# Expert gate sums as one fp32 product per token and half, and the low parts of the down weights on VectorE

## The chip, the cores and the metric

The kernel runs on one core of a Trainium2 chip. The metric is the device time of one execution in microseconds; 2326.19 us is the median of three runs of the kernel before, from 2315.31 to 2331.83. The core has TensorE (matrix products into PSUM), VectorE, ScalarE and GpSimd (element-wise work on 128 partitions), SyncE (which here starts most transfers) and DMA engines.

## The reference, cut to what matters

The program computes two transformer blocks on 256 tokens of width 1024. The first block has an attention branch and a state-space branch, and then a layer of experts; the second block has neighbourhood attention, a gated recurrence and feed-forward layers. The change lies in the layer of experts and in nothing else:

```python
def peer_ffn(xn, w_q, keys1, keys2, u_tab, v_tab):
    q = (xt @ w_q).reshape(T, PEER_HEADS, PEER_QDIM)
    s1 = jnp.einsum('thd,hkd->thk', q[..., :half], keys1)
    s2 = jnp.einsum('thd,hkd->thk', q[..., half:], keys2)
    v1, i1 = lax.top_k(s1, PEER_TOPK)
    v2, i2 = lax.top_k(s2, PEER_TOPK)
    cand = v1[..., :, None] + v2[..., None, :]
    cidx = i1[..., :, None] * PEER_NKEYS + i2[..., None, :]
    sv, pos = lax.top_k(cand, PEER_TOPK)
    eidx = jnp.take_along_axis(cidx, pos, axis=-1)
    gw = jax.nn.softmax(sv, axis=-1)
    ...
    act = jnp.einsum('td,thkd->thk', xc, jnp.take(u_tab, ec, axis=0))
    hact = jax.nn.gelu(act, approximate=False) * gc
    return jnp.einsum('thk,thkd->td', hact, jnp.take(v_tab, ec, axis=0))
```

Each of 8 heads picks 16 of 128 x 128 = 16384 experts for each token, with weights gw. An expert is a row of u_tab and a row of v_tab.

## The kernel before, in words

The kernel does not gather experts. It computes the activations of all 16384 experts for all 256 tokens, multiplies each by the sum of the weights with which the token picked it (zero for most), and multiplies the result by all of v_tab. The experts are numbered (i1, i2); the tile A holds the activations as [i2, i1, token], in two halves of i1 with 64 values each.

The steps of the layer are these.

- The selection (`topk`) finds on VectorE the indices i1 and i2 and the weight of each of the 128 picks (8 heads x 16) of each token. At its end TensorE transposes them, so that the picks lie on partitions; `iT` holds i1, i2 and the weight, as three bf16 parts whose sum is the weight.
- The up part (`u_blocks`) takes one block of 128 experts after the other, 128 blocks. SyncE loads 512 KB of u_tab; ScalarE makes the high part of each weight (`whi`, line 1024), and VectorE or GpSimd the low part (`wlo`, line 1025); TensorE runs 24 products of 256 columns (high by high, high by low, low by high for eight chunks, lines 227 to 229); ScalarE applies the gelu (line 1037).
- The gate sums (`gates(half)`, lines 999 to 1015) run in 32 steps of 8 tokens for each half. For each token the sum over picks is a product of two matrices: one has a one where a pick's i2 equals the row (`oa`, line 1004), the other the weight where the pick's i1 equals the column (`ob`). VectorE compares a repeated index `iox` with i2 (128x1024, line 1004) and with i1 (128x512, line 1005, tile `eqw`), and multiplies the second by each of the three parts of the weight (line 1008, three times). TensorE then adds three bf16 products of 64 columns for each of 8 tokens (line 1012), and VectorE multiplies the sums into A (line 1014). `oa` has two buffers (one inside the tile C8, so that the trace calls it C), `ob` two, and the sums two banks of PSUM.
- The down part (`v_blocks`) goes over 128 blocks again. SyncE loads 512 KB of v_tab, ScalarE makes `whi` (line 1045), VectorE or GpSimd `wlo` (line 1046, by the set POOL_V), and the activations of the block are split in the same way: `wwh` on ScalarE (line 217) and `wwl` on VectorE (line 222), 256 columns each, with two buffers. TensorE runs 12 products of 512 columns for a block (lines 308, 309 and 312); those of line 312 read `wwl`. `wraw`, `whi` and `wlo` have three buffers each, and a block's weights are split two blocks ahead.
- Beside all this stand the modulation sums of the second block (`ada`, line 180): products of 128x1024 on VectorE with a sum along the row.

The order on each engine is not written by hand. The program is written step after step, with `even` dealing the steps of the selection, of the gate sums and of the modulation among the blocks; a scheduler of the build then puts the instructions of each engine into one queue by its own estimate of when each is ready. Each engine runs its queue in order. The gate sums of the first half (`gates(0)`) are dealt among up blocks 76 to 127, those of the second half (`gates(1)`) among the first 64 down blocks:

```python
    for i, _ in enumerate(u_blocks(76, 128)):
        even(g0, i, 32, 50)
...
    for i, _ in enumerate(v_blocks(0, 64)):
        even(g1, i, 32, 60)
        even(ada1, i, 40, 64)
```

In the queues the first gate step stands well ahead of up block 76, since the selection is expected to end earlier.

The names P, V, S, G and Q are TensorE, VectorE, ScalarE, GpSimd and SyncE.

Of the kernel before, what the change touches and what calls it, by code (L numbers as in the profile page):

```python
# [14 lines left out]
OP = mybir.AluOpType  # L15
# [9 lines left out]
def constants():  # L25
    """Arrays that depend on shapes alone."""
# [27 lines left out]
# Parameter vectors that are used as columns of 128: name, input, columns  # L54
# [6 lines left out]
def tiles(w, n=256):  # L61
    """w [R, C] in blocks of 512 rows and n columns, [C / n, R / 512, 128, 4 n]: rows of a block in four chunks of 128"""
    r, c = w.shape
    return w.reshape(r // 512, 4, 128, c // n, n).transpose(3, 0, 2, 1, 4).reshape(c // n, r // 512, 128, 4 * n)


def lay_out(inputs):
    """The inputs, in the order in which they are loaded"""
# [16 lines left out]
def program(tc, I, out, C, taps=None, upto=99):  # L85
# [44 lines left out]
    def col(name, i=0, n=1):  # L130
        """Column i.. of a parameter; a digit or two after the name picks the row of a stacked one."""
# [13 lines left out]
    def prepare_cols():  # L145
# [5 lines left out]
        # half the convolution: silu(y) = y / 2 (1 + tanh y / 2)  # L151
# [5 lines left out]
    msc = cst.tile([128, 5, 8], F32, name="msc")             # (1 + scale) * norm weight  # L157
    mods = cst.tile([128, 14, 8], F32, name="mods")      # layer 0: 0..5, layer 1: 6..11, context: 12, 13

    def ada(chunks, cs, raws, junk=None):  # L160
        """chunks of (layer, chunk, [(slot, which)]): mods[:, slot] = silu(c) @ ada_w chunk + ada_b chunk, as columns.
        cs(which): silu(c) as a row on all partitions"""
# [26 lines left out]
    def to_row(slot, src):  # L189
        """Columns src [128, 8] also as a row"""  # L190
# [7 lines left out]
    def row(dst, slot):  # L198
        """The row on all partitions"""
        Q.dma_start(dst, bass.AP(tensor=rowed[slot].tensor, offset=0, ap=[[0, 128], [1, D]]))  # L200
# [5 lines left out]
    pool_every = [0, 0]                                  # every n-th weight unit has its low part made by GpSimd  # L206

    after = []                                           # weights are split after these
# [22 lines left out]
    # Streamed weights: units of [128, 1024]; a phase may add buffers of its own to the rotation.  # L231
# [23 lines left out]
    def load_up(W, c0, u0=0):  # L255
        """Columns c0.. of W in tiles: two units of [128, 4, n]."""
# [10 lines left out]
    def load_dn(W, k0, gate=None, n=2, bufs=()):  # L267
        """Rows 128 k0 .. of W [K, 1024], with its columns times the gate: n units of [128, 1024]."""
# [11 lines left out]
    def up_T(units, cg, h, ps, k0=0, nk=8, start=True, stop=True):  # L280
        """ps[128 cols, 256 t] += W[:, cg].T @ h^T"""
# [6 lines left out]
    def up_N(units, tt, h, ps):  # L288
        """ps[128 t, 256 cols] = h @ W[:, 256 cols]"""
# [5 lines left out]
    def down(units, hk, acc, start, stop, free=False, tts=(0, 1), norm=None):  # L295
        """acc[tt][half][128 t, 512] += h^T[k].T @ W[k rows, 1024] for the units and their (hi, lo) [128, 256].
        At the stop the sums are finished one after the other, and the norm of them begins between.
        Free: the sums go on growing after they were read."""
# [40 lines left out]
    def start_acc(acc, x, ident):  # L339
        """Opens the sums with the residual x [128, 2, 1024]."""  # L340
# [7 lines left out]
    def rsqrt(v, mul, add):  # L348
        """v [128, n] -> 1 / sqrt(v * mul + add), in place"""
# [11 lines left out]
    def warm(src):  # L361
        """Has ScalarE's table for Sqrt loaded once src is there."""
# [4 lines left out]
    def keep_clock(ins=None, n=12):  # L367
        """Work without a result after ins: the tensor engine's clock falls when it waits."""
# [7 lines left out]
    class Norm:  # L376
        """src(tt, half) [128, 512] natural -> h = (hi, lo) [128, 8, 256] of (rms(x) * scale + shift)^T, in steps"""
# [6 lines left out]
        def stat(self, tt, hf):  # L384
            """Sums of squares"""
# [43 lines left out]
    class Output(Norm):  # L429
        """The final norm"""  # L430
# [14 lines left out]
    def nat_T(src, h, nchunk, scale=None):  # L445
        """src(tt, c) [128 t, 128] -> h = (hi, lo) [128, nchunk, 256]"""
# [13 lines left out]
    def mix(main, side, per=1):  # L460
        """Emit steps of side between the steps of main."""
# [1261 lines left out]
```

## Time and profile before

| what | value |
|---|---|
| median of three runs | 2326.19 us |
| lowest and highest run | 2315.31 and 2331.83 us |
| span of the profiled execution | 2330.2 us |
| TensorE busy (matmul) | 2223.8 us, 95% of the span |
| VectorE busy | 1678.7 us, 72% |
| ScalarE busy | 1013.8 us, 44% |
| GpSimd busy | 919.8 us, 39% |

The profile is of one execution; its span goes from the first to the last instruction. PE stands for TensorE's products, PEld for its weight loads, DVE for VectorE, ACT for ScalarE, POOL for GpSimd and SPq for SyncE's queue. L1012 is line 1012 of the kernel before. A product's duration in the profile holds the time it takes to pass through the array, so that the products of a run overlap; what one costs is read from the distance of two starts. An fp32 product stands in the trace as two records, each with a weight load of its own, where one in the reduced fp32 form (fp32r) or in bf16 has one. An instruction's time can include a wait for access that no semaphore shows.

### The profile page before, as it was taken

What the parts mean: (1) busy time and instruction counts of PE and PEld (TensorE: products, weight loads), DVE (VectorE), ACT (ScalarE), POOL (GpSimd) and SP (SyncE); (2) the same over time, 40 slices, a digit from 0 to 9 for tenths busy, and PEclk for the clock granted to TensorE, in tenths of its full rate; (3) what the DMA queues carried; (4) which work ended last, traced back from release to release, by engine and by line L of the source; (5) the groups of instructions that cost most, each with busy time, mean ns of one, the idle gap of its engine ahead of it and who ended that gap; (6) DMA issues with size and microseconds to landing.
All of it is one profiled execution on the core that took longest, in us unless ns stands there. A gap on an engine that the chain in (4) does not pass through costs nothing.

```text
span 2330.2 us, 39435 instructions
## 1 busy us (share of the span) xinstructions
PE 2223.8 (95%) x15750; PEld 2048.7 (88%) x15750; DVE 1678.7 (72%) x2726; ACT 1013.8 (44%) x1666; POOL 919.8 (39%) x439
## 2 busy tenths in 40 slices
PE   9999999998789999999999999999988899999999
PEld 8999998898789999997888877789977799888998
DVE  6677688699996553439887698643677687777876
ACT  5555664443234332223333345544542455444554
POOL 2222342205456533324434443442242355353654
PEclk9999999999899999999999999999999999999999
DMA  6544443566456543336555587775521555554552
GB/s 202 165 127 139 156 132 110 175 196 202 147 175 204 188 146 108 109 111 241 174 188 190 194 320 263 244 163 102 82 83 46 190 184 196 177 185 135 191 200 99
DMA packets 108218, 386.90 MB, mean 166 GB/s; under 512 B 13026, under 2 KB 14066, under 8 KB 108035
## 3 DMA queue, kind: packets, MB, share of 16 engines
q1 hardware_dynamic: 106080, 380.04, 48.8%
q0 software_dynamic: 1520, 3.75, 2.6%
q8 instruction: 123, 2.02, 0.3%
q10 hardware_dynamic: 434, 0.59, 0.1%
q14 instruction: 61, 0.49, 0.1%
HBM read 382.18 MB, written 2.16 MB: 165 GB/s over the span
## 4 chain that ended last, share of the span: by engine, by line
PE 73%; DVE 16%; DMA 4%; issue 3%; ACT 2%; POOL 1%; SPq 0%; ACTq 0%; DVEq 0%; POOLq 0%
PE mm L227 14%; PE mm L228 13%; PE mm L229 13%; PE tr L1012 7%; PE acc L312 6%; PE acc L309 5%; PE acc L308 5%; DVE A L180 2%; DMA wraw<-in_peer_v 2%; DVE wlox L222 1%; DVE xdt L180 1%; POOL wlo L1046 1%; DMA xdt<-in_ada_w 1%; DVE ob L1008 1%; PE acc L227 1%
## 5 line engine op out<-in xcount | busy, mean ns | idle before, releaser
L229 PE MATMUL mm<-xdt,wlo 128*128 128x256 f32 x1248 | 363.8, 292 | 29.6 <-DVE wlo L1025 29.2
L227 PE MATMUL mm<-xdt,whi 128*128 128x256 f32 x1248 | 370.6, 298 | 5.0 <-ACT A L1037 3.5
L1025 POOL TENSOR_TENSOR wlo<-wraw,whi 128x1024 fp32r<-128x1024 f32 x93 | 237.2, 2554 | 325.2 <-ACT whi L1024 323.2
L228 PE MATMUL mm<-xdt,whi 128*128 128x256 f32 x1152 | 336.8, 292 | 0.2 <-DVE xdt L418 0.2
L1046 POOL TENSOR_TENSOR wlo<-wraw,whi 128x1024 fp32r<-128x1024 f32 x80 | 208.6, 2609 | 288.2 <-ACT whi L1045 270.2
L1024 ACT ACTIVATE whi<-wraw 128x1024 fp32r<-128x1024 f32 x128 | 136.0, 1062 | 337.7 <-PE mm L228 156.3
L229 PEld LDWEIGHTS mm<-xdt,wlo 128*128 128x128 f32 x1248 | 249.9, 200 | 30.8 <-DVE wlo L1025 30.2
L227 PEld LDWEIGHTS mm<-xdt,whi 128*128 128x128 f32 x1248 | 250.6, 201 | 6.5 <-ACT A L1037 4.2
L228 PEld LDWEIGHTS mm<-xdt,whi 128*128 128x128 f32 x1152 | 231.2, 201 | 0.4 <-DVE xdt L418 0.4
L222 POOL TENSOR_TENSOR wlo<-wraw,whi 128x1024 fp32r<-128x1024 f32 x37 | 93.8, 2536 | 277.9 <-ACT whi L217 241.2
L309 PE MATMUL acc<-wlo,wwh 128*128 128x512 f32 x512 | 175.1, 409 | 3.2 <-DVE wlo L1046 2.5
L308 PE MATMUL acc<-whi,wwh 128*128 128x512 f32 x512 | 167.0, 410 | 1.1 <-ACT whi L1045 1.1
L312 PE MATMUL acc<-whi,wwl 128*128 128x512 f32 x512 | 158.1, 406 | 9.5 <-DVE wwl L222 9.4
L222 DVE TENSOR_TENSOR wlo<-wraw,whi 128x1024 fp32r<-128x1024 f32 x87 | 130.8, 1504 | 50.2 <-ACT whi L217 49.6
L1045 ACT ACTIVATE whi<-wraw 128x1024 fp32r<-128x1024 f32 x128 | 135.9, 1062 | 69.9 <-DMA wraw<-in_peer_v 40.4
L227 PE MATMUL mm<-F,whix 128*128 128x256 f32 x560 | 158.3, 283 | 8.0 <-ACT whix L217 5.7
L217 ACT ACTIVATE whi<-wraw 128x1024 fp32r<-128x1024 f32 x124 | 130.7, 1055 | 72.0 <-PE mm L228 35.4
L228 PE MATMUL mm<-F,whix 128*128 128x256 f32 x560 | 158.2, 283 | 0.4 <-DVE F L418 0.4
L229 PE MATMUL mm<-F,wlox 128*128 128x256 f32 x560 | 157.9, 282 | 0.5 <-DVE wlox L222 0.5
L1014 DVE TENSOR_TENSOR A<-A,tr 128x512 f32<-128x512 f32 x64 | 43.8, 686 | 153.4 <-PE tr L1012 151.5
L217 ACT ACTIVATE wwh<-A 128x256 fp32r<-128x256 f32 x128 | 53.1, 416 | 222.5 <-PE acc L309 188.4
L275 POOL TENSOR_TENSOR wrawx<-wrawx,grow 128x1024 f32<-128x1024 f32 x38 | 106.1, 2803 | 88.3 <-DMA wrawx<-in_ffn_w_down 56.0
(611 smaller groups left out, 6810.1 us busy)
## 6 DMA issues: line engine op xcount, KB each, us to landing
wraw<-in_peer_u SPq DMA_DIRECT2D x128, 512.0 KB, 3.7
wraw<-in_peer_v SPq DMA_DIRECT2D x128, 512.0 KB, 4.1
xdt<-in_ada_w SPq DMA_DIRECT2D x72, 512.0 KB, 5.0
wraw<-in_ffn_w_up SPq DMA_DIRECT2D x56, 512.0 KB, 4.2
wraw<-in_w_in SPq DMA_DIRECT2D x42, 512.0 KB, 3.7
wrawx<-in_ffn_w_up SPq DMA_DIRECT2D x32, 512.0 KB, 7.6
wrawx<-in_ffn_w_down SPq DMA_DIRECT2D x31, 512.0 KB, 4.8
wrawx<-in_w_in SPq DMA_DIRECT2D x30, 512.0 KB, 3.6
```

The lines of the kernel that those rows point to most:

```text
L217: S.activation(hi, raw, AF.Copy)
L222: eng.tensor_tensor(lo, raw, hi.bitcast(F32), op=OP.subtract)
L227: P.matmul(ps, ah, bh, start=start, stop=False)
L228: P.matmul(ps, ah, bl, start=False, stop=False)
L229: P.matmul(ps, al, bh, start=False, stop=stop)
L308: P.matmul(acc[tt][hf], ah, hi[:, fs], start=st_, stop=False, skip_group_check=free)
L309: P.matmul(acc[tt][hf], ah, lo[:, fs], start=False, stop=False, skip_group_check=free)
L312: P.matmul(acc[tt][hf], al, hi[:, fs], start=False, stop=sp_ and not free, skip_group_check=free)
L1012: P.matmul(pg[:, t], oa[:, :, t], ob[:, j, :, t], start=j == 0, stop=j == 2)
L1024: S.activation(hi, raw, AF.Copy)
L1025: (G if b in POOL_U else V).tensor_tensor(lo, raw, hi.bitcast(F32), op=OP.subtract)
L1046: (G if b in POOL_V else V).tensor_tensor(lo, raw, hi.bitcast(F32), op=OP.subtract)
```

## The change

The gate sums are computed with fp32 operands. `iT` keeps i1, i2 and the whole weight in fp32. A step compares the index with i2 over 128x1024 and with i1 over 128x512, both in fp32 with tokens outermost, and multiplies the second by the weight in place, once. TensorE runs one fp32 product per token and half, 8 a step, where it ran 24. The repeated index `iox` and the small operations that made the parts of the weight go. The set POOL_V becomes empty: VectorE makes all 128 low parts of the down weights, where GpSimd made 80.

```diff
-    wk = keep.tile([128, 4 * D], BF, name="C8")
-    iT = wk[:, 0:1280].rearrange("p (j t) -> p j t", j=5)
-    iox = wk[:, 1280:2304].rearrange("p (i t) -> p i t", t=8)
-    eqw = wk[:, 2304:2816].rearrange("p (i t) -> p i t", t=8)
-    oas = itertools.cycle([wk[:, 2816:3840].rearrange("p (i t) -> p i t", t=8),
-                           wrk.tile([128, 128, 8], BF, name="oa", bufs=1)])
-    iota = wk[:, 3840:4096].bitcast(F32)
+    wk = keep.tile([128, 2 * D], F32, name="C8")
+    iT = wk[:, 0:768].rearrange("p (j t) -> p j t", j=3)
+    iota = wk[:, 768:896]
+    oas = itertools.cycle([wk[:, 896:1920].rearrange("p (t i) -> p t i", t=8),
+                           wrk.tile([128, 8, 128], F32, name="oa", bufs=1)])
     G.dma_start(iota, C["iota"])
-    V.tensor_copy(iox, iota.unsqueeze(2).to_broadcast([128, 128, 8]))
...
-            V.tensor_copy(iT[:, 0:3, ts], pt.rearrange("p (j t) -> p j t", j=3))
-            rest = flat(102, 1)[:, 128:256]
-            V.tensor_tensor(rest, pt[:, 256:384], iT[:, 2, ts], op=OP.subtract)
-            V.tensor_copy(iT[:, 3, ts], rest)
-            V.tensor_tensor(iT[:, 4, ts], rest, iT[:, 3, ts], op=OP.subtract)
+            V.tensor_copy(iT[:, :, ts], pt.rearrange("p (j t) -> p j t", j=3))
             yield
 
     def gates(half):
-        hs = slice(half * 64, half * 64 + 64)
+        io = iota.unsqueeze(1).to_broadcast([128, 8, 128])
+        ioh = iota[:, half * 64:half * 64 + 64].unsqueeze(1).to_broadcast([128, 8, 64])
         for t0 in range(0, T, 8):
             ts = slice(t0, t0 + 8)
-            oa, eq = next(oas), eqw
-            V.tensor_tensor(oa, iox, iT[:, 1, ts].unsqueeze(1).to_broadcast([128, 128, 8]), op=OP.is_equal)
-            V.tensor_tensor(eq, iox[:, hs], iT[:, 0, ts].unsqueeze(1).to_broadcast([128, 64, 8]), op=OP.is_equal)
-            ob = wrk.tile([128, 3, 64, 8], BF, name="ob")
-            for j in range(3):
-                V.tensor_tensor(ob[:, j], eq, iT[:, 2 + j, ts].unsqueeze(1).to_broadcast([128, 64, 8]), op=OP.mult)
+            oa = next(oas)
+            V.tensor_tensor(oa, io, iT[:, 1, ts].unsqueeze(2).to_broadcast([128, 8, 128]), op=OP.is_equal)
+            ob = wrk.tile([128, 8, 64], F32, name="ob")
+            V.tensor_tensor(ob, ioh, iT[:, 0, ts].unsqueeze(2).to_broadcast([128, 8, 64]), op=OP.is_equal)
+            V.tensor_tensor(ob, ob, iT[:, 2, ts].unsqueeze(2).to_broadcast([128, 8, 64]), op=OP.mult)
             pg = ps_tr((128, 8, 64))
             for t in range(8):
-                for j in range(3):
-                    P.matmul(pg[:, t], oa[:, :, t], ob[:, j, :, t], start=j == 0, stop=j == 2)
+                P.matmul(pg[:, t], oa[:, t], ob[:, t], start=True, stop=True)
...
-    POOL_V = set(b for b in range(1, 64) if b % 4) | set(range(65, 128, 2))
+    POOL_V = ()
```

The change moves instructions, since the build orders the queues anew. On TensorE, in the first half of the down part, the queue before has in one place (acc are the sums of the down products, tr the gate sums, C_6360 and oa the two buffers of the i2 comparison):

```order
9021 L308 MATMUL acc<-whi,wwh 128x512
9022 L309 MATMUL acc<-wlo,wwh 128x512
9023 L1012 LDWEIGHTS C_6360
9024 L1012 MATMUL tr<-ob,C_6360 128x64
9025 L312 MATMUL acc<-whi,wwl 128x512 x4
9026 L1012 LDWEIGHTS C_6360
9027 L1012 MATMUL tr<-ob,C_6360 128x64
```

There the gate products of a step, 24 pairs of such rows, stand on both sides of a block's last products, or whole between two blocks. After the change the same part of the queue reads:

```order
7021 L1006 MATMUL tr<-ob,C_6360 128x64 x8
7022 L312 MATMUL acc<-whi,wwl 128x512 x4
7023 L308 MATMUL acc<-whi,wwh 128x512 x4
7024 L309 MATMUL acc<-wlo,wwh 128x512 x4
7025 L312 MATMUL acc<-whi,wwl 128x512 x4
7026 L308 MATMUL acc<-whi,wwh 128x512 x4
7027 L309 MATMUL acc<-wlo,wwh 128x512 x4
7028 L1006 MATMUL tr<-ob,oa 128x64 x8
7029 L312 MATMUL acc<-whi,wwl 128x512 x4
```

The eight products of a step stand now ahead of the four products that read `wwl`, and there are two blocks from step to step. On VectorE, in the same part, the queue before reads (A_5787 is the second half of the activations, xdt the modulation weights):

```order
1246 L1046 TENSOR_TENSOR wlo<-wraw,whi 128x1024
1247 L180 SCALAR_TENSOR_TENSOR xdt,mods<-xdt 128x1024
1248 L222 TENSOR_TENSOR wwl<-A_5786,wwh 128x256
1249 L1014 TENSOR_TENSOR A_5787<-A_5787,tr 128x64x8
1250 L1004 TENSOR_TENSOR oa<-C_6360 128x1024
1251 L1008 TENSOR_TENSOR ob<-C_6360 128x512 x3
1252 L180 SCALAR_TENSOR_TENSOR xdt,mods<-xdt 128x1024
1253 L222 TENSOR_TENSOR wwl<-A_5786,wwh 128x256
```

Here a low part of the weights comes once in some four blocks. After the change VectorE's queue reads in that part:

```order
1241 L1003 TENSOR_TENSOR ob<-ob,C_6360 128x512
1242 L1008 TENSOR_TENSOR A_5787<-A_5787,tr 128x64x8
1243 L1000 TENSOR_TENSOR C_6360<-C_6360 128x1024
1244 L1002 TENSOR_TENSOR ob<-C_6360 128x512
1245 L222 TENSOR_TENSOR wwl<-A_5786,wwh 128x256
1246 L1040 TENSOR_TENSOR wlo<-wraw,whi 128x1024
1247 L222 TENSOR_TENSOR wwl<-A_5786,wwh 128x256
1248 L1040 TENSOR_TENSOR wlo<-wraw,whi 128x1024
1249 L180 SCALAR_TENSOR_TENSOR xdt,mods<-xdt 128x1024
1250 L1003 TENSOR_TENSOR ob<-ob,C_6360 128x512
```

A gate step has four operations where it had six, a low part of the weights stands behind each low part of the activations, and the multiplied one-hots of a step (line 1003) come last, behind both. The instructions behind the last down blocks are the same as before and stand in the same order on every engine, but for a few neighbours on TensorE and SyncE.

## Rows read from the trace of the kernel before

**Rows 1.** Busy time by stretch: PE, PEld, DVE, ACT, POOL, PEclk, DMA share, GB/s.

```profile
690.00:1037.00 347.00, 345.85 (x2757) 342.59 (x2756) 178.72 (x266) 111.34 (x168) 147.79 (x59) 0.96 0.44 145
1040.00:1323.00 283.00, 279.04 (x1506) 230.72 (x1505) 225.97 (x347) 91.01 (x123) 123.81 (x47) 0.95 0.58 198
1323.00:1523.00 200.00, 189.83 (x823) 152.40 (x821) 152.07 (x194) 101.49 (x147) 83.38 (x34) 0.98 0.77 268
```

**Rows 2.** Groups of TensorE, 690 to 1037: xcount, busy us, mean ns, idle before.

```profile
L229 PE MATMUL mm<-xdt,wlo 128*128 128x256 f32 x662 | 192.7, 291 | 1.2 <-DVE wlo L1025 1.2
```

**Rows 3.** Timeline of TensorE around one gate step: start us, us, instruction.

```profile
887.69 0.28 PE L229 MATMUL mm<-xdt,wlo 128*128 128x256 f32 x1
887.81 3.12 PE L1012 MATMUL tr<-ob,oa 128*128 128x64 bf16 x24
890.68 0.37 PE L227 MATMUL mm<-xdt,whi 128*128 128x256 f32 x1
```

**Rows 4.** A group of TensorE, 1040 to 1323, and timeline rows of one block.

```profile
L309 PE MATMUL acc<-wlo,wwh 128*128 128x512 f32 x240 | 92.9, 422 | 0.0
...
1120.16 1.07 PE L308 MATMUL acc<-whi,wwh 128*128 128x512 f32 x4
1121.06 1.07 PE L309 MATMUL acc<-wlo,wwh 128*128 128x512 f32 x4
```

**Rows 5.** Timeline of TensorE in the attention, fp32 by fp32.

```profile
179.01 0.33 PE L598 MATMUL acc<-B,pT 128*128 128x64 f32 x2
179.18 0.39 PE L599 MATMUL acc<-B,pT 128*128 128x64 f32 x2
179.40 0.39 PE L600 MATMUL acc<-B,pT 128*128 128x64 f32 x2
```

**Rows 6.** Timeline of VectorE at the end of the selection and later.

```profile
676.17 1.21 DVE L973 TENSOR_TENSOR A<-A,C 128x1024 f32<-128x1024 f32 x1
...
680.25 0.68 DVE L1004 TENSOR_TENSOR C<-C 128x1024 bf16<-128x1024 bf16 x1
680.84 0.41 DVE L1005 TENSOR_TENSOR C<-C 128x512 bf16<-128x512 bf16 x1
...
855.73 1.09 DVE L1008 TENSOR_TENSOR ob<-C 128x512 bf16<-128x512 bf16 x3
856.74 1.22 DVE L1025 TENSOR_TENSOR wlo<-wraw,whi 128x1024 fp32r<-128x1024 f32 x1
```

**Rows 7.** Groups of VectorE, two from 1040 to 1323, the last 690 to 1037.

```profile
L180 DVE SCALAR_TENSOR_TENSOR xdt<-xdt 128x1024 f32<-128x1024 f32 x41 | 58.3, 1424 | 0.3 <-DMA xdt<-in_ada_w 0.3
L222 DVE TENSOR_TENSOR wwl<-A,wwh 128x256 fp32r<-128x256 f32 x60 | 42.3, 707 | 25.1 <-PE acc L312 14.8 <-ACT wwh L217 10.3
...
L1014 DVE TENSOR_TENSOR A<-A,tr 128x512 f32<-128x512 f32 x32 | 21.9, 688 | 121.6 <-PE tr L1012 119.7 <-ACT A L1037 1.9
```

**Rows 8.** Timeline of GpSimd and VectorE, 1099 to 1104.

```profile
1099.54 2.56 POOL L1046 TENSOR_TENSOR wlo<-wraw,whi 128x1024 fp32r<-128x1024 f32 x1
...
1099.78 2.60 DVE L222 TENSOR_TENSOR wwl<-A,wwh 128x256 fp32r<-128x256 f32 x1
...
1103.45 0.41 DVE L222 TENSOR_TENSOR wwl<-A,wwh 128x256 fp32r<-128x256 f32 x1
```

**Rows 9.** Groups of GpSimd, 690 to 1037, 1040 to 1323, 1323 to 1523.

```profile
L1025 POOL TENSOR_TENSOR wlo<-wraw,whi 128x1024 fp32r<-128x1024 f32 x59 | 147.8, 2507 | 191.1 <-ACT whi L1024 191.1
...
L1046 POOL TENSOR_TENSOR wlo<-wraw,whi 128x1024 fp32r<-128x1024 f32 x47 | 125.3, 2670 | 171.6 <-ACT whi L1045 171.2 <-DVE C L1005 0.4
...
L1046 POOL TENSOR_TENSOR wlo<-wraw,whi 128x1024 fp32r<-128x1024 f32 x34 | 85.6, 2518 | 119.5 <-ACT whi L1045 101.9 <-DVE wlo L1046 6.1 <-DVE F L408 3.0
```

**Rows 10.** Busy time by stretch, the later part of the gate sums' first half.

```profile
890.00:1037.00 147.00, 147.00 (x1127) 145.79 (x1126) 62.12 (x125) 38.05 (x58) 44.56 (x19) 0.92 0.32 101
```

**Rows 11.** Groups of TensorE and VectorE, 1323 to 1523.

```profile
L312 PE MATMUL acc<-whi,wwl 128*128 128x512 f32 x263 | 77.5, 399 | 5.6 <-DVE wwl L222 5.5
...
L222 DVE TENSOR_TENSOR wwl<-A,wwh 128x256 fp32r<-128x256 f32 x65 | 48.9, 761 | 19.5 <-PE acc L312 14.2 <-PE tr L193 2.9 <-ACT wwh L217 2.3
```

## The prediction

> **What bounds the kernel now.** On the page's first part TensorE is by far the busiest engine. The change touches only the expert layer, so the view to read is the engines' busy time by stretch [rows 1]. I cut it at three stretches: G0 (690 to 1037 us, up blocks beside the gate sums of the first half), G1 (1040 to 1323, down blocks beside the gate sums of the second half) and V (1323 to 1523, down blocks alone). In G0 TensorE is busy 345.9 of 347 us and VectorE 179, in G1 279 of 283 and VectorE 226, in V 190 of 200 and VectorE 152. So TensorE sets the pace in G0 and G1, but in G1 VectorE is not far behind.
>
> What TensorE does there can be counted. In G0 it runs 662 products of each of three kinds [rows 2], eight of each to an up block: 83 blocks of 24, one every 0.12 us, 2.88 us a block [rows 3]. Beside them stand 32 gate steps of 24 bf16 products; one step takes 887.81 to 890.68, 2.87 us [rows 3]. 83 x 2.88 + 32 x 2.87 = 331 of the 347 us. In G1 240 products of each kind, four to a down block, are 60 blocks [rows 4]; four start in 0.90 us, so a block is 12 x 0.225 = 2.70. 60 x 2.70 + 32 x 2.87 = 254 of the 283 us.
>
> **The gate sums on TensorE.** Before, eight tokens cost 24 products and 2.87 us. After, they cost 8 products of fp32 operands with 128x128 weights and 64 columns. The trace has that form in the attention: L598 to L600 multiply fp32 by fp32, 128 by 64 columns, each product in two records, and the next pair starts 0.17 and then 0.22 us later [rows 5]. I take 0.22, since the pair in the middle has its like on both sides. 8 x 0.22 = 1.76, so a step loses 1.11 us, and 32 steps 35.5 us, in G0 and again in G1. Bounds: at 0.17 a product a step takes 1.36, and a half gains 48 us; at double the 0.22 it loses, which is a rival below.
>
> A rule stands against this. The Trainium skill (TensorE: Matmul & The Clock Gate, Weight-path perf modes) says that the fast way of loading weights is open to types other than fp32 only. By an estimate from it, with fp32 loads twice as long as the 0.12 us between bf16 gate products, a step of 16 records would take 3.84 us and a half would be 31 us slower. The rows say 0.11 us between fp32 records [rows 5], so here the trace does not bear it out.
>
> **The gate sums on VectorE.** Before, a step is one comparison over 1024 columns in bf16 (0.68), one over 512 (0.41), three multiplications (1.09 together) [rows 6] and the multiplication into the activations (0.69) [rows 7]. Each starts some 0.07 to 0.09 before the last has ended, so the step takes 0.60 + 0.34 + 1.01 + 0.61 = 2.56 us. After, the comparison is fp32 with a value repeated along the columns, as L973 is: 1.21 [rows 6], 1.14 from start to start. The two over 512 columns have no row; 256 columns of that kind take 0.41 [rows 8] and 1024 take 1.21, so I take 0.67, 0.60 from start to start, bounds 0.34 and 1.14. With 0.61 for the last: 1.14 + 0.60 + 0.60 + 0.61 = 2.95, 0.39 more a step, 12 us a half. In G0 this lies beside TensorE: VectorE waits 121.6 us there, nearly all for gate products [rows 7]. The cast that built the repeated index and six small operations at the end of the selection go too; they lie beside up blocks, and I count nothing (bounds 3 us either way).
>
> **The low parts.** GpSimd makes 47 of them in G1 at 2.67 us [rows 9]; VectorE's own take 1.22 [rows 6]. The two engines exclude each other: when GpSimd's subtraction ran from 1099.54 to 1102.10, VectorE's 256-column one took 2.60 us instead of 0.41 [rows 8]. That is why the mean of that group is 707 ns in G1 [rows 7]. With GpSimd out of G1 and V, these waits end. VectorE's own work in G1 becomes: 60 low parts x 1.15 = 69, 60 of the 256-column ones x 0.34 = 20, 41 modulation sums [rows 7] x 1.15 = 47, 32 gate steps x 2.95 = 94, together 230 us. TensorE's is 162 + 32 x 1.76 = 218. So VectorE becomes the longer of the two, by little.
>
> The order says how closely they are coupled: VectorE makes the multiplied one-hots, then ends an earlier step, prepares the next one, and alternates two low parts of activations with two of weights; TensorE has two blocks a step. The 256-column subtraction waits for the block two before, and the low part of the weights now stands in the same queue, behind the gate operations. Between a step's multiplied one-hots and the next 256-column subtraction VectorE spends 0.61 + 1.14 + 0.60 + 0.34 = 2.69 us, TensorE 1.76 on the gate products: if VectorE has no lead, TensorE waits 0.93 us once a step, 30 us over 32 steps. Its buffers allow it a lead of a block or two, so I take a third of that, 10: 240 for G1 against 283, 43 gained. Bounds: 230 at the lower end, no gain at the upper.
>
> In G0 the granted clock is 0.92 from 890 on [rows 10], a loss of some 0.08 x 147 = 12 us. There whole runs of 24 gate products stand between up blocks. With shorter runs between 0 and 12 may come back; I take 4. Against it, GpSimd still makes low parts in G0 (59, 148 us [rows 9]), and VectorE's longer operations wait for it more often: I take 5. G0 gains 35.5 + 4 - 5 = 35.
>
> In V TensorE loses 5.6 us, nearly all to the 256-column subtraction, whose mean is 761 ns there [rows 11] against 0.41 alone. GpSimd's waits go, and 34 low parts [rows 9] x 1.15 = 39 us come to a VectorE that is busy 152 of 200 us, waits included. The transfers move 268 GB/s at a share of 0.77 [rows 1], so I take 6 us gained, bounds 12 and -6.
>
> **The sum.** 35 + 43 + 6 = 84 us. The profiled execution spans 2330.2 us, 4 above the median of the runs: 2246 on its scale, 2242 on theirs (what lies around its span is not shown and taken as the same). What follows V has the same instructions.
>
> **The rivals.**
> VectorE becomes the bound in G1 and gives the gain back. Its idle time there is 283 - 226 = 57 us, nearly all spent waiting for TensorE; if the taking of turns stays, G1 is 230 + 57 = 287, 4 lost, V gives nothing, and G0 its 35: 31 gained, 2295. For it speaks the single queue, against it that most of this idle time comes from TensorE being the bound.
>
> The shared access holds up G0. VectorE's 179 us there grow by 12, and with GpSimd's 148 [rows 1] make 339, waits for one another included, in a stretch of 312. If TensorE then waits for one-hots or low parts, about half of the 35 goes: 2260. Against it, TensorE loses only 1.2 us to low parts there now [rows 2].
>
> On the other side: the fp32 product costs double. If each needs four records of 0.11 for its four partial products, it costs 0.44, a step 3.52 against 2.87, 21 us more in each half; less the 6 in V, 36 us slower, 2362. It decides from 2.87 / 8 = 0.36 us a product on. Against it stand the two records of L599.
> The Trainium skill (FP8 and Floating Point Precision, TensorE Precision Notes) says that true fp32 takes four passes through the array. By that rule a product of 64 columns streams 256; the rows show two records for it, and whether each holds two passes they don't say.
>
> **How the numbers follow.** Forecast 0.70, VectorE bound in G1 0.16, shared access 0.08, fp32 at double cost or VectorE far worse 0.06. The forecast's own range is 2215 (G1 at 230, the clock wholly back, 12 in V) to 2275. The whole range goes from 2205, which adds the spread of the runs, to 2300, which takes in the first rival. A measurement tells about 1% from no change, 23 us: half of the first rival falls within that, so faster 0.86, same 0.08, slower 0.06.
>
> **What would show it.** Right: two records a gate product at 0.11 us, G0 some 312 us and G1 some 240 long, VectorE busy nearly all of G1, the 256-column group near 0.41 us in G1 and V, TensorE's waits in V gone. Wrong: four records a product; G1 near 283 with TensorE waiting for one-hots or low parts; G0 with waits for VectorE.

## The result and the profile after

The changed kernel takes 2231.32 us (median of four runs, 2227.15 to 2232.76); the kernel before, run beside it, 2329.01 (2315.31 to 2333.28). The ratio is 0.958, with a 95% interval from 0.955 to 0.961: 98 us less, where 84 were forecast. The profiled execution spans 2228.9 us against 2330.2.

The stretches are read again between the same marks: G0 from the first gate product to the last up product, G1 from there to the last gate product, V from there to the point where four down blocks are left (those four take 11 us in both). Busy time by stretch, kernel after (columns as in [rows 1]):

```profile
693.00:997.50 304.50, 299.26 (x2508) 298.98 (x2507) 193.75 (x192) 110.24 (x167) 146.42 (x59) 0.99 0.53 164
997.50:1238.50 241.00, 238.81 (x1294) 202.93 (x1292) 233.12 (x344) 95.73 (x129) 0.00 (x0) 1.00 0.73 243
1238.50:1420.00 181.50, 173.19 (x747) 137.32 (x746) 137.26 (x216) 91.83 (x139) 1.26 (x8) 0.99 0.82 276
```

By the same marks before, G0 went from 690.3 to 1041.1, G1 to 1323.6 and V to 1517.7 us. So G0 fell from 350.8 to 304.5 (46 less), G1 from 282.5 to 240.9 (42 less), V from 194.1 to 181.1 (13 less); what lies ahead and behind changes by some 3 us each. G1 now holds 64 down blocks where it held 60 (L312 has 256 records there, against 240). At [rows 4]'s 2.70 us a block these four are 11 us, so with equal blocks G1 gained 52 or 53 and V 2. The granted clock, 0.96 and 0.95 in [rows 1], is 0.99 and 1.00.

What a gate step costs, on the timeline (start us, us, instruction), two rows of G0 and some of G1:

```profile
989.97 1.90 PE L1006 MATMUL tr<-ob,oa 128*128 128x64 f32 x16
991.67 0.36 PE L227 MATMUL mm<-xdt,whi 128*128 128x256 f32 x1
...
1126.21 0.68 DVE L1003 TENSOR_TENSOR ob<-ob,C 128x512 f32<-128x512 f32 x1
1126.82 0.67 DVE L1008 TENSOR_TENSOR A<-A,tr 128x512 f32<-128x512 f32 x1
1127.41 1.21 DVE L1000 TENSOR_TENSOR oa<-C 128x1024 f32<-128x1024 f32 x1
1128.16 1.89 PE L1006 MATMUL tr<-ob,C 128*128 128x64 f32 x16
1128.55 0.67 DVE L1002 TENSOR_TENSOR ob<-C 128x512 f32<-128x512 f32 x1
1129.15 0.40 DVE L222 TENSOR_TENSOR wwl<-A,wwh 128x256 fp32r<-128x256 f32 x1
```

Eight products are 16 records, two a product, and the next product starts 1.70 us after the first of them: 0.21 a product, where the forecast took 0.22. VectorE's step is 0.61 + 0.59 + 1.14 + 0.60 = 2.94 us from start to start, against 2.95 forecast.

Who waits: groups of the kernel after, TensorE in G0, G1 and V, then VectorE in G0 (two), G1 (two) and V (two):

```profile
L1006 PE MATMUL tr<-ob,oa 128*128 128x64 f32 x256 | 31.7, 276 | 5.2 <-DVE C L989 5.2
...
L312 PE MATMUL acc<-whi,wwl 128*128 128x512 f32 x256 | 72.4, 403 | 1.9 <-DVE wwl L222 1.8
...
L312 PE MATMUL acc<-whi,wwl 128*128 128x512 f32 x240 | 66.2, 397 | 5.1 <-DVE wwl L222 5.0
...
L1000 DVE TENSOR_TENSOR oa<-C 128x1024 f32<-128x1024 f32 x16 | 34.1, 2132 | 0.3 <-PE tr L1006 0.3
L1008 DVE TENSOR_TENSOR A<-A,tr 128x512 f32<-128x512 f32 x32 | 21.9, 687 | 64.6 <-PE tr L1006 62.7 <-ACT A L1031 1.9
...
L1040 DVE TENSOR_TENSOR wlo<-wraw,whi 128x1024 fp32r<-128x1024 f32 x65 | 79.0, 1216 | 8.6 <-ACT whi L1039 8.6
L222 DVE TENSOR_TENSOR wwl<-A,wwh 128x256 fp32r<-128x256 f32 x62 | 25.7, 415 | 0.0
...
L180 DVE SCALAR_TENSOR_TENSOR xdt<-xdt 128x1024 f32<-128x1024 f32 x29 | 35.5, 1225 | 33.4 <-DMA xdt<-in_ada_w 33.4
L222 DVE TENSOR_TENSOR wwl<-A,wwh 128x256 fp32r<-128x256 f32 x62 | 25.9, 419 | 3.0 <-PE acc L312 2.8 <-PE tr L193 0.2
```

The 256-column subtraction takes 415 ns in G1 where it took 707 [rows 7]: GpSimd is silent there. In G0, where GpSimd still works, the comparison over 1024 columns takes 2132 ns on the mean instead of the 1210 of the timeline above, but VectorE has 64.6 us to spare and TensorE waits for none of it but 5.2 us at the very first step, for the copy of the picks. In V the subtraction is at 419 as well, yet TensorE waits as long for it as before, 5.0 us against 5.5 [rows 11].

### The profile page after: what moved, and what is told of

It reads as the page before. It is cut to its first block, busy times and chain, and to the rows that moved or that the text cites. A ratio compares the mean times of both kernels' runs of the same rounds, so it can differ in the third digit from the quotient of the medians.

```text
span 2228.9 us, 38314 instructions
## 1 busy us (share of the span) xinstructions
PE 2124.5 (95%) x15238; PEld 1966.2 (88%) x15238; DVE 1697.8 (76%) x2671; ACT 1011.9 (45%) x1666; POOL 714.6 (32%) x359
## 4 chain that ended last, share of the span: by engine, by line
PE 66%; DVE 21%; DMA 7%; issue 4%; ACT 2%; SPq 0%; POOL 0%; DVEq 0%; ACTq 0%
PE mm L227 13%; PE mm L228 13%; PE mm L229 13%; PE acc L309 5%; PE acc L312 5%; PE acc L308 4%; PE tr L1006 4%; DMA xdt<-in_ada_w 3%; DVE A L180 2%; DVE wlo L1040 2%; DVE wlo L222 1%; DMA wraw<-in_peer_v 1%; DVE xdt L180 1%; DVE wlox L222 1%; DVE wlo L1019 1%
## 5 line engine op out<-in xcount | busy, mean ns | idle before, releaser
L229 PE MATMUL mm<-xdt,wlo 128*128 128x256 f32 x1248 | 358.9, 288 | 28.7 <-DVE wlo L1019 28.3
L227 PE MATMUL mm<-xdt,whi 128*128 128x256 f32 x1248 | 362.8, 292 | 5.0 <-ACT A L1031 3.6
L1019 POOL TENSOR_TENSOR wlo<-wraw,whi 128x1024 fp32r<-128x1024 f32 x93 | 241.6, 2600 | 282.1 <-ACT whi L1018 278.3
L228 PE MATMUL mm<-xdt,whi 128*128 128x256 f32 x1152 | 331.0, 287 | 0.2 <-DVE xdt L418 0.2
L229 PEld LDWEIGHTS mm<-xdt,wlo 128*128 128x128 f32 x1248 | 244.8, 196 | 29.9 <-DVE wlo L1019 29.1
L227 PEld LDWEIGHTS mm<-xdt,whi 128*128 128x128 f32 x1248 | 244.2, 196 | 6.5 <-ACT A L1031 4.2
L228 PEld LDWEIGHTS mm<-xdt,whi 128*128 128x128 f32 x1152 | 226.5, 197 | 0.4 <-DVE xdt L418 0.4
L222 POOL TENSOR_TENSOR wlo<-wraw,whi 128x1024 fp32r<-128x1024 f32 x37 | 92.7, 2505 | 308.6 <-ACT whi L217 271.9
L222 DVE TENSOR_TENSOR wlo<-wraw,whi 128x1024 fp32r<-128x1024 f32 x87 | 136.8, 1573 | 50.6 <-ACT whi L217 50.1
L1040 DVE TENSOR_TENSOR wlo<-wraw,whi 128x1024 fp32r<-128x1024 f32 x128 | 155.8, 1218 | 15.8 <-ACT whi L1039 15.8
L312 PE MATMUL acc<-whi,wwl 128*128 128x512 f32 x512 | 142.9, 400 | 7.1 <-DVE wwl L222 6.8
L308 PE MATMUL acc<-whi,wwh 128*128 128x512 f32 x512 | 145.3, 395 | 0.5 <-ACT wwh L217 0.5
L309 PE MATMUL acc<-wlo,wwh 128*128 128x512 f32 x512 | 144.2, 392 | 0.4 <-DVE wlo L1040 0.3
L312 PEld LDWEIGHTS acc<-whi,wwl 128*128 128x128 f32 x512 | 92.5, 188 | 31.1 <-DVE wwl L222 13.7
```

Source lines behind the costliest of these rows:

```text
L222: eng.tensor_tensor(lo, raw, hi.bitcast(F32), op=OP.subtract)
L227: P.matmul(ps, ah, bh, start=start, stop=False)
L228: P.matmul(ps, ah, bl, start=False, stop=False)
L229: P.matmul(ps, al, bh, start=False, stop=stop)
L308: P.matmul(acc[tt][hf], ah, hi[:, fs], start=st_, stop=False, skip_group_check=free)
L309: P.matmul(acc[tt][hf], ah, lo[:, fs], start=False, stop=False, skip_group_check=free)
```

## The experiments

### The two edits apart, and the low parts alone once more

The kernel before with the second edit alone, and the kernel after with the second edit undone:

```diff
 # low parts alone
-    POOL_V = set(b for b in range(1, 64) if b % 4) | set(range(65, 128, 2))
+    POOL_V = ()
 # gates alone
-    POOL_V = ()
+    POOL_V = set(b for b in range(1, 64) if b % 4) | set(range(65, 128, 2))
```

> The kernel before with the low parts of the down weights all on VectorE; the gate sums stay three bf16 products. Theory (TensorE's products carry the gain): TensorE still has 60 x 2.70 + 32 x 2.87 = 254 us in G1 and loses some 14 to the clock, so G1 goes from 283 to about 270 and V loses some 10: about 20 us faster than before, 2309. Rival (GpSimd's share of the access was the bound of G1): G1 falls to VectorE's 218 or so, some 60 us faster, 2265.

> The changed kernel with GpSimd's low parts of the down weights as before (80 of 128). Theory: G0 is as in the changed kernel (some 46 us shorter than before); in G1 VectorE's 230 - 47 x 1.15 = 176 us, less 20 that read PSUM, and GpSimd's 47 x 2.4 = 113 exclude each other, 269 us, so G1 stays at about 270 and V as before: some 58 us faster than before, 2270. Rival (the two edits add up, no exclusion worth a term): G1 falls to TensorE's 218 plus some 15, together 95 faster, 2235.

Measured: low parts alone 2337.43 us, ratio 0.999 (0.996 to 1.002); gates alone 2289.43, ratio 0.980 (0.974 to 0.986); before, beside both, 2335.79. So the edits give nothing and 46 us by themselves and 98 together. Both runs are slower than their theories expected, 2309 and 2270.

With the gates alone, G0 is what it is after the whole change (303.8 us), and G1 is 278.2, hardly shorter than the 282.5 of before and 8 more than expected. Busy time by stretch, gates alone, G1:

```profile
996.50:1274.70 278.20, 243.88 (x1246) 202.70 (x1244) 266.27 (x288) 90.78 (x123) 129.00 (x47) 0.94 0.59 199
```

Groups of the same run, TensorE and VectorE in G1:

```profile
L309 PE MATMUL acc<-wlo,wwh 128*128 128x512 f32 x240 | 97.6, 415 | 5.0 <-DVE wlo L1040 5.0
L312 PE MATMUL acc<-whi,wwl 128*128 128x512 f32 x240 | 81.1, 422 | 28.2 <-DVE wwl L222 28.2
...
L1002 DVE TENSOR_TENSOR ob<-C 128x512 f32<-128x512 f32 x30 | 46.5, 1549 | 0.0
L222 DVE TENSOR_TENSOR wwl<-A,wwh 128x256 fp32r<-128x256 f32 x60 | 46.3, 775 | 11.2 <-ACT wwh L217 8.5 <-PE acc L312 2.7
```

VectorE is busy 266 of 278 us because GpSimd's 47 low parts stretch its instructions (1549 ns for the 512-column comparison that takes 670 in the changed kernel), TensorE waits 33 us for it, and the granted clock is 0.94. In the kernel before the same stretching was there [rows 7], but TensorE lost only 4.0 us to it, since its own gate products were the longer work. Group of TensorE, kernel before, G1:

```profile
L312 PE MATMUL acc<-whi,wwl 128*128 128x512 f32 x240 | 78.0, 415 | 4.0 <-DVE wwl L222 3.9
```

That is why the second edit is worth nothing ahead of the first, and after it 58 us by the medians (51 by the ratios to the kernel before that ran beside each).

But low parts alone should still have won those 4 us and some. Busy time by stretch, low parts alone, two pieces of G1:

```profile
1051.00:1300.00 249.00, 249.00 (x1267) 208.67 (x1266) 196.97 (x335) 93.07 (x127) 0.00 (x0) 0.95 0.67 229
...
1315.00:1356.00 41.00, 33.17 (x228) 29.42 (x227) 25.39 (x58) 1.08 (x3) 0.00 (x0) 0.50 0.07 27
```

Of the first 64 down blocks 60 are done by 1294 us and all by 1310; VectorE's queue has their splits ahead of the last gate steps, of which ten are left then. These run with little beside them, on a clock of 0.50, that is 1.2 GHz, for 41 us: 20 us lost. To test this, VectorE's splits of a block were queued behind the one-hots of the gate step dealt before it, with nothing else changed:

```diff
+            made.append(last)
...
-            if b < 126:
-                vt[b + 2] = v_split(b + 2)
...
-            split(blk(b), wh, wl)
+            with tc.issue_after(made[-1].ins):
+                if b < 126:
+                    vt[b + 2] = v_split(b + 2)
...
+                split(blk(b), wh, wl)
```

> The kernel before with all low parts of the down weights on VectorE, as in the run that gave 2337 us, but in VectorE's queue the splits of a down block stand behind the one-hots of the last gate step that is dealt before it. In that run the queue ran all 64 first down blocks ahead of the last 11 gate steps, and TensorE, left with the steps alone, stood at half its clock for 41 us (20 us lost). Theory (the low parts' gain was eaten by this tail): the gate steps spread again, the 41 us at half clock go, and the time is near 2337 - 20 = 2317. Rival (TensorE's own work bounds the stretch, with its clock lost elsewhere in the same amount): 2330 to 2340, as before.

Measured: 2318.05 us, ratio 0.995 (0.992 to 0.998), against 2331.59 beside it. Busy time by stretch of this run, G1:

```profile
1049.00:1331.00 282.00, 281.79 (x1510) 236.38 (x1509) 222.33 (x397) 91.44 (x124) 0.00 (x0) 0.94 0.59 201
```

The stretch at half clock is gone, G1 ends 19 us earlier, and the low parts alone are worth 0.5%. TensorE is busy in all of G1: with bf16 gate products it is the bound, whoever makes the low parts. In both of these runs G0 was 12 to 14 us longer than before, with a clock of 0.93 against 0.96, over instructions that the edit does not touch; so 0.5% may be less than the edit is worth by itself.

### What bounds G1 now

From the changed kernel, in the second half only: without the multiplication by the weight on VectorE, or with four of the eight products on TensorE.

```diff
 # less for VectorE
-            V.tensor_tensor(ob, ob, iT[:, 2, ts].unsqueeze(2).to_broadcast([128, 8, 64]), op=OP.mult)
+            if half == 0:
+                V.tensor_tensor(ob, ob, iT[:, 2, ts].unsqueeze(2).to_broadcast([128, 8, 64]), op=OP.mult)
 # less for TensorE
-                P.matmul(pg[:, t], oa[:, t], ob[:, t], start=True, stop=True)
+                if half == 0 or t < 4:
+                    P.matmul(pg[:, t], oa[:, t], ob[:, t], start=True, stop=True)
```

> The changed kernel; left out are the 32 multiplications of the one-hots by the weight in the second half (the output is then that of weights of one there). VectorE has 32 x 0.60 = 19 us less in G1. Theory (TensorE and VectorE are both full in G1, TensorE 7.23 us a step, VectorE 7.1): G1 shrinks by 5 us at most. Rival (VectorE alone is the bound): G1 shrinks by 19.

> The changed kernel; left out are four of the eight gate products of each step in the second half (the sums of the first four tokens serve for the others). TensorE has 32 x 0.89 = 28 us less in G1, VectorE the same work. Theory (both full): G1 shrinks by 5 to 10 us, to VectorE's 230 to 235. Rival (TensorE alone is the bound): G1 shrinks by 28.

Measured, one run each: 2225.55 and 2222.26 us, 6 and 9 less than the changed kernel (11 and 15 by the ratio to the kernel before, 2335.79 beside these), for 19 us of VectorE's work (32 x 0.60) and 27 of TensorE's (32 x 0.85). Busy time by stretch, G1, less for VectorE and then less for TensorE:

```profile
994.00:1225.50 231.50, 228.08 (x1244) 193.10 (x1242) 207.65 (x299) 90.17 (x123) 0.00 (x0) 1.00 0.70 237
...
992.00:1231.50 239.50, 217.86 (x1031) 178.20 (x1030) 231.41 (x341) 94.72 (x128) 0.00 (x0) 0.97 0.71 240
```

The first holds 60 down blocks and the second 63. With 64, as in the changed kernel, at 2.70 us a block both would take 242 us, against 240.9 there. So neither relief shortens G1, and the 5 to 10 us expected of the second did not come. The 6 and 9 us lie elsewhere, 3 of each in G0 (301.5 us against 304.5), which these edits do not touch. Relieve TensorE and it only waits more (busy 217.9 of 239.5), since VectorE stays nearly full at 231; relieve VectorE (busy 208) and TensorE is full, at 228 of 231.5. The two engines are level there; neither alone gives anything.

Sixteen of the 64 low parts of G1 given back to GpSimd (`POOL_V = set(range(2, 64, 4))`):

> The changed kernel with 16 of the first 64 low parts of the down weights on GpSimd. Theory (exclusion): VectorE loses 16 x 1.15 = 18 us of work, and gains waits of up to 16 x 2.4 = 38 us, and it is full: G1 grows by 5 to 20 us. Rival (any work off VectorE helps, as GpSimd is idle in G1): G1 shrinks by 3 to 10 us.

Measured: 2242.36 us, ratio 0.962 (0.956 to 0.968), 11 more than the changed kernel. G1 holds 60 blocks; at equal blocks it is 14 us longer, as the theory expected. Busy time by stretch, G1:

```profile
997.50:1242.00 244.50, 231.09 (x1245) 194.12 (x1243) 236.35 (x314) 90.38 (x123) 43.75 (x15) 0.99 0.65 223
```

Groups of VectorE and TensorE there:

```profile
L222 DVE TENSOR_TENSOR wwl<-A,wwh 128x256 fp32r<-128x256 f32 x59 | 37.6, 640 | 5.3 <-ACT wwh L217 3.9 <-PE acc L312 1.4
...
L312 PE MATMUL acc<-whi,wwl 128*128 128x512 f32 x240 | 71.5, 405 | 9.8 <-DVE wwl L222 9.8
```

A quarter of the low parts on GpSimd takes the subtraction from 415 to 640 ns and TensorE's wait from 1.8 to 9.8 us. VectorE was relieved of 16 x 1.15 = 18 us of work and is busy longer, 236 us for 60 blocks against 233 for 64: what GpSimd takes over costs VectorE more in waits for access than it saves.

### What bounds V

Half of the low parts of the last 64 blocks back on GpSimd (`POOL_V = set(range(65, 128, 2))`):

> The changed kernel with 32 of the last 64 low parts of the down weights on GpSimd, as before the change; none in the first 64. Theory (GpSimd's subtraction holds up VectorE's 256-column one, which TensorE waits for): V grows by 6 to 14 us, the mean of the 256-column group goes from 419 to some 750 ns. Rival (V is bound by its transfers): the same time within 3 us.

Measured: 2232.89 us, ratio 0.958 (0.953 to 0.964): no difference from the changed kernel. Busy time by stretch of this run in V, then groups, TensorE, VectorE and ScalarE:

```profile
1237.50:1419.00 181.50, 174.01 (x747) 139.69 (x746) 145.72 (x184) 94.64 (x138) 75.31 (x30) 0.97 0.79 272
...
L312 PE MATMUL acc<-whi,wwl 128*128 128x512 f32 x240 | 70.2, 401 | 3.6 <-DVE wwl L222 3.4
...
L222 DVE TENSOR_TENSOR wwl<-A,wwh 128x256 fp32r<-128x256 f32 x61 | 52.9, 881 | 12.8 <-PE acc L312 9.2 <-ACT wwh L217 3.6
...
L1039 ACT ACTIVATE whi<-wraw 128x1024 fp32r<-128x1024 f32 x59 | 62.6, 1061 | 36.8 <-DMA wraw<-in_peer_v 20.9 <-PE acc L312 15.0
```

And the ScalarE group of the kernel after, same stretch:

```profile
L1039 ACT ACTIVATE whi<-wraw 128x1024 fp32r<-128x1024 f32 x60 | 63.7, 1062 | 71.3 <-DMA wraw<-in_peer_v 66.0 <-PE acc L312 5.3
```

The subtraction goes back to 881 ns, V stays 181.5 us long, and TensorE waits 3.4 us for it, not more than the 5.0 of the changed kernel. So the stretched subtraction is not what holds V. Without GpSimd the split of the weights merely waits longer for its transfer, 66.0 us instead of 20.9, which points to the transfers, as the rival has it: V moves 272 and 276 GB/s in the two. But that is not the most that they can give. The run of the next section that has each gate product twice went through 66 blocks of this part at 2.80 us each, against 3.02 here, with TensorE never idle:

```profile
1330.00:1515.00 185.00, 184.90 (x827) 152.09 (x827) 146.85 (x229) 102.40 (x149) 1.26 (x8) 1.00 0.81 291
```

In V itself TensorE is busy 173 and 174 of 181.5 us, so its own products make up most of the length. Where the other 8 us come from is not shown; no run changed the transfers.

### What a gate product costs, and a cheaper one

Each product of the changed kernel run twice, in both halves:

```diff
+            for t in range(8):
+                P.matmul(pg[:, t], oa[:, t], ob[:, t], start=True, stop=True)
```

> The changed kernel with each gate product issued twice (the same result), 32 records of a step in place of 16. Price: at 0.112 us a record a step takes 1.79 us more, G0 and G1 grow by 57 us each where TensorE bounds them, 2231 + 114 = 2345. Clock: if the falls of the granted clock come with the length of a run of gate products (3.6 us now, 2.9 before the change, 1.8 after), they come back, 10 us or more lost in G0 and G1 together on top, 2355 or more. If they came with the bf16 products as such, the clock stays at 0.99 to 1.00 in both stretches.

Measured, one run: 2321.37 us, 90 more. Busy time by stretch:

```profile
694.00:1047.50 353.50, 353.50 (x3022) 353.48 (x3022) 178.14 (x193) 111.12 (x168) 145.01 (x59) 1.00 0.41 142
1047.50:1330.00 282.50, 282.50 (x1757) 251.03 (x1755) 233.94 (x335) 90.11 (x122) 0.00 (x0) 1.00 0.54 198
```

G0 grew by 353.2 - 304.5 = 49 us. The changed kernel lost 3 us there to the clock and 5 to waiting, and this run neither, so the products cost 57 us, 57 / 32 / 8 = 0.22 us each. G1 grew by 52 at equal blocks; V, at 2.80 us a block, was 13 us shorter, which the sum of 2345 did not have. And the clock is full throughout, though a step's gate products now stand 3.5 us in a row, as the timeline of TensorE in G0 shows:

```profile
902.71 1.90 PE L1006 MATMUL tr<-ob,C 128*128 128x64 f32 x16
904.44 1.95 PE L1008 MATMUL tr<-ob,C 128*128 128x64 f32 x16
906.20 0.36 PE L227 MATMUL mm<-xdt,whi 128*128 128x256 f32 x1
```

So a long row of gate products does not by itself lower the clock. What else changed with the type is the layout: before, eight tokens lay innermost, so that one token's columns were eight bf16 values apart; now a token's columns are adjacent. The last test keeps bf16 and all 24 products of the kernel before, and the low parts on VectorE, and puts the tokens innermost in pairs instead of eights:

```diff
-    iox = wk[:, 1280:2304].rearrange("p (i t) -> p i t", t=8)
+    iox = wk[:, 1280:1536].rearrange("p (i w) -> p i w", w=2)
...
-            V.tensor_tensor(oa, iox, iT[:, 1, ts].unsqueeze(1).to_broadcast([128, 128, 8]), op=OP.is_equal)
+            def pick(j, n):
+                return iT[:, j, ts].rearrange("p (q w) -> p q w", w=2).unsqueeze(2).to_broadcast([128, 4, n, 2])
+            V.tensor_tensor(oa, iox.unsqueeze(1).to_broadcast([128, 4, 128, 2]), pick(1, 128), op=OP.is_equal)
...
-                    P.matmul(pg[:, t], oa[:, :, t], ob[:, j, :, t], start=j == 0, stop=j == 2)
+                    P.matmul(pg[:, t], oa[:, t // 2, :, t % 2], ob[:, j, t // 2, :, t % 2], start=j == 0, stop=j == 2)
```

> All low parts of the down weights on VectorE, and the gate sums as three bf16 products again, but with the one-hots laid out in pairs of tokens: a product's weights and columns then lie 2 elements apart in place of 8, and VectorE's inner stretch is two elements. If the 0.12 us between bf16 gate products came from the step of 8 elements, it falls to about the 0.06 of bf16 products with adjacent weights in the state-space branch (L752): a step takes 24 x 0.06 = 1.44 us, G0 and G1 lose some 11 us each against the changed kernel, 2210. If it came from bf16 weights as such, the time is that of the kernel with the low parts alone moved, about 2309. If VectorE's operations lose their speed on stretches of two, a step costs it 4.3 us in place of 2.56, and G1 grows to some 275: 2260.

Measured: 2189.00 us, ratio 0.939 (0.933 to 0.945): 42 us below the changed kernel. Timeline of TensorE in G1:

```profile
1060.43 0.89 PE L1014 MATMUL tr<-ob,C 128*128 128x64 bf16 x24
1061.15 1.17 PE L309 MATMUL acc<-wlo,wwh 128*128 128x512 f32 x4
```

The same 24 products that took 2.87 us [rows 3] take 0.72, 0.03 each, half of the 0.06 expected; only the distance of the columns differs, in both operands, and which of the two counts was not separated. VectorE's operations keep their speed (0.68 and 0.41 us, as in [rows 6]). Busy time by stretch, G0:

```profile
692.00:966.00 274.00, 269.76 (x2762) 266.56 (x2762) 218.37 (x265) 109.96 (x167) 148.07 (x59) 0.99 0.53 180
```

Most of the gain over the changed kernel lies here, 31 us, where VectorE has time to spare; G1, where it has hardly any, is 238 us for 64 blocks against 241, and V 7 us shorter. The Trainium skill (Advanced Engine Details and Errata, SBUF Cachelines) says that accesses are at full speed while they fall into the same 16 bytes, at least two of them, and are penalised when each falls into another. The trace agrees: eight bf16 values are 16 bytes and two are 4, with 0.12 and 0.03 us a product.

This version, too, ends G1 with gate steps alone, from 1170 us on, when the first 64 blocks are done; busy time by stretch:

```profile
1157.00:1204.00 47.00, 29.30 (x316) 23.69 (x315) 43.61 (x91) 6.05 (x8) 0.00 (x0) 0.66 0.49 181
```

It was run with the queue rule above, and, without that rule, with GpSimd's low parts as in the kernel before:

> The version with the three bf16 products and the one-hots in pairs of tokens (2189 us), with the same rule for VectorE's queue. Its 11 last gate steps too stood alone, 47 us with TensorE busy 29 and VectorE 44. Theory (VectorE bounds the second half with these cheap products): the tail goes, but its VectorE work only moves forward among the blocks; 2180 to 2189, mostly the clock that is not lost. Rival (the tail was TensorE's waiting and is won back whole): near 2165.

> The version with pairs of tokens, with GpSimd making 80 low parts of the down weights as in the kernel before. Theory (the two edits depend on each other: the cheaper the gate products, the more the waits between GpSimd and VectorE cost): the 98 us that lie between the two fp32 runs with either set, 2289 and 2231, come back as 58 or more, so 2247 to 2265. Rival (the edits add up, and low parts are worth nothing as they were in the kernel before): near 2189.

Measured: in turn 2184.13 us, ratio 0.938 (0.933 to 0.942), the fastest here, though its interval overlaps that of the pairs without the rule. With GpSimd's low parts 2239.32, ratio 0.961 (0.956 to 0.965), 50 us above the pairs: the theory's kind of loss, a little under its 58 (the 98 in its text should read 58, the distance from 2231 to 2289). TensorE's group in G1 of that last run:

```profile
L312 PE MATMUL acc<-whi,wwl 128*128 128x512 f32 x240 | 83.9, 441 | 37.7 <-DVE wwl L222 37.6
```

The cheaper the gate products, the longer TensorE waits for a VectorE that shares with GpSimd: 3.9 us before, 28.2 with fp32, 37.6 with pairs. The first and the last differ in the layout of the one-hots alone.

## Why the prediction was right, and where its sizes were off

**The gate sums on TensorE: right.** Two records a product, 0.21 us against 0.22. A step went from 2.87 to 1.70: 37 us a half against 35.5. The rival of double cost fell with the first row.

**G0: 35 forecast, 46 measured.** 37 come from the products. The term that was mis-sized is the clock: 4 us were taken out of a possible 12, and the loss went from 14 (0.04 x 351) to 3, nearly all back. The prediction saw the low clock where whole steps of gate products stood in a row, and expected shorter runs to help a little. From 850 us on the steps still stand whole, 1.70 us each, and doubled to 3.5 us they did no harm; what went with the low clock was the bf16 product in its old layout, and why is not shown. The 5 us for waits between GpSimd and VectorE did not come: VectorE's instructions were stretched as feared (2132 ns), but its 65 us of spare time hid all of it. TensorE's idle time grew by 4 us, at the first step. 37 + 11 - 4 = 44; 2 are not accounted for.

**G1: 43 forecast, 52 at equal blocks.** 240 us were forecast for 60 blocks and 240.9 measured for 64. Of the 52, 37 are products, 14 the clock (0.05 x 283, now 1.00), about 2 less waiting. The sum had no term for the clock in G1 although [rows 1] shows 0.95 there; it was put together from VectorE's side, 230 and 10 of waiting. Those 10 us that TensorE was to wait for VectorE's queue came to 2, so G1 is at its lower bound of 230 for 60 blocks. That this bound held is partly luck. TensorE's 218 left out 12 us of its busy time (238.8 measured, against 64 x 2.70 + 32 x 1.70 = 227), and with them it came out just level with VectorE, as the runs with less work for either showed. With both halves together the clock gave back some 25 us where the sum had 4, more than the 14 us between forecast and result.

**V: 6 forecast, 2 measured.** The subtraction fell to 419 ns as forecast, and TensorE's waits did not go. The failed step reads [rows 11] as one cause: 5.5 us of waiting for an instruction stretched by GpSimd. With the stretching gone or put back, V is equally long and TensorE waits 5.0 and 3.4 us for that instruction, so the stretching is not the cause; what the cause is stays open.

**The rivals.** VectorE giving the gain back in G1 did not happen in the changed kernel, but it is what the gates alone did (278.2 us), where GpSimd stretches VectorE's instructions; the second edit is what removed that. The prediction summed that edit inside G1 and did not price the edits apart; by themselves they are worth 0 (or 13 us in a better order) and 46 us. The Trainium skill's rule that fp32 gets no fast weight load (TensorE: Matmul & The Clock Gate, Weight-path perf modes) was judged against 0.12 us a bf16 product. That row was no measure of bf16: at a distance of two elements it is 0.03 against 0.106 for an fp32 record, which the rule would lead one to expect. The forecast stands on rows of fp32, so it was not touched, but the conclusion that fp32 loads cost no more than bf16 ones was wrong.

## What to carry to other kernels

Before replacing products by a costlier type, look at what one costs from start to start and at the distance of its columns in memory: a 64-column product at 0.12 us was slow for its layout, and mending that gained 42 us more than changing the type. Judge an edit that frees a waiting engine in the state in which it will stand: the same edit was worth nothing, or 50 us and more, by how long TensorE's own work was. A wait that a profile names is not always won back by speeding up what it names: in V the subtraction took little more than half the time and the wait stayed, and in G1 work taken off one of two level engines gave nothing.

## What the runs showed of the hardware

The granted clock went with the kind and the order of the products. In the kernel before it was full while gate products stood in fives and sixes between up products, and fell where whole steps stood in a row. Busy time by stretch, kernel before:

```profile
695.00:850.00 155.00, 154.77 (x1281) 153.32 (x1282) 94.84 (x103) 59.95 (x90) 87.56 (x35) 1.00 0.58 194
850.00:1040.00 190.00, 190.00 (x1468) 188.46 (x1468) 80.58 (x160) 49.11 (x75) 57.23 (x24) 0.93 0.32 101
```

TensorE waits for nothing from 850 on, and the clock is 0.93. With the same steps in fp32, with twice as many of them, and with bf16 in pairs, the clock over this part of G0 is 1.00. The kernel after:

```profile
850.00:997.00 147.00, 147.00 (x1254) 146.98 (x1254) 104.78 (x112) 48.12 (x75) 55.15 (x23) 1.00 0.44 130
```

It fell in other places too: to 0.50 where bf16 steps of the old layout stood alone, to 0.66 where steps in pairs did, and to 0.94 and 0.97 in G1 where TensorE waited for VectorE (gates alone, less for TensorE). Why it was lower in G0 in both runs with the low parts moved (0.87 and 0.89 from 850 on, one execution each) stays open.

That eight fp32 products of the same shape as those of the attention cost what [rows 5] said was expected; that 24 bf16 products can be had in less than half of their time, and a quarter of their own, by the distance of the columns alone, was not.
